# The second matrix product of a gated convolution layer, done by seven products on 2x2 blocks like the first

## The chip, the cores and the metric

The kernel runs on one core of one Trainium2 chip. The metric is the device time of one execution in microseconds, as the median of several runs. Before the change it is 1654.18 us (three runs, 1650.93 to 1654.26).

The engines are named as in the profile: PE is TensorE's matmuls and PEld its weight loads, DVE is VectorE, ACT is ScalarE, POOL is GpSimd, and SP is the engine whose queue issues nearly all DMAs here.

## The reference

One layer of a decoder trunk, batch 1, 2048 tokens, 1024 channels, all in float32:

```
shift, scale, gate = split(silu(c) @ ada_w + ada_b, 3)
h = rmsnorm(x) * (1 + scale) + shift                 # 2048 x 1024
u, gc, gb, z = split(h @ w_in, 4)                    # first product: 2048x1024 by 1024x8192
v = gc * u
y = gb * (causal_conv3(v) + conv_b) * silu(z)        # 2048 x 2048, each channel by itself
out = rmsnorm(x + gate * (y @ w_out), final_g)       # second product: 2048x2048 by 2048x1024
```

## The kernel before

Each float32 operand of a product is split into a high part in the type fp32r and a low part, what the high part leaves (`split`: ACT casts the high part, DVE subtracts). A product of two operands is three matmuls: low by high, high by high, high by low.

**First product.** It runs in two halves of the tokens (`hf` 0 and 1; 1024 tokens each). Its operands are cut into 2x2 blocks, and the four output blocks come from seven block products, not eight. The stationary side (`w`) are sums of blocks of `w_in` (`Weights`: two tiles `raw` of 512 KB for a group, the sums S1 to S4 on DVE, then seven splits). The moving side (`b`) are sums of blocks of `h`: 7 operands of 4 tiles of 512 KB, 28 tiles that stay in SBUF through a half. A group `g` (32 in a half) is seven products in the order 1, 6, 7, 5, 2, 4, 3, each of 12 matmuls of 512 columns, added up in four PSUM banks A to D: products 1 and 2 share A, 7 and 4 share D, 5 and 3 share C. `Pair.take` reads a bank when a product is done, so product 4 can't start before DVE has read D after product 7, nor product 3 before it has read C after product 5.

The moving tiles come from the pool `op`, with 33 buffers; 28 of them hold `b`. The operands of the second half are made during the first half (`make_second`, a side job of some steps, run between products) and kept in DRAM (`op_d`). They replace those of the first half during its last group, tile by tile, as each product there has used its own for the last time.

The convolution and the gating (`Mixer.finish`) write `y` to DRAM (`y_d`), channel block by channel block, with channels on partitions.

**Second product.** For each of 16 tiles of 128 tokens, `y` is loaded from `y_d` and split (`load_y`), and `mm_out` runs over 16 channel blocks, two halves of the output columns and three matmuls of 512 columns: 96 matmuls for a token tile, 1536 in all, with y as the stationary side. `w_out` is split on the way through the first two tiles and stays in SBUF. `finish` multiplies with the gate, adds x, and normalizes.

**Order.** A scheduler sets the order on each engine from dependencies, its own estimates of durations, and free buffers. `prepare(n + AHEAD)` puts the split of a stationary operand four products ahead. Engines run their instructions in order. SP's queue is in order too: a DMA that waits holds up those behind it, and each waits for the end of the one issued eight earlier (the semaphores DMAHW0 to DMAHW7).

Of the kernel before, what the change touches and what calls it, by code (L numbers as in the profile page):

```python
# [18 lines left out]
def trunk_kernel(ctx: ExitStack, tc: tile.TileContext, x, c, final_g, ada_w, ada_b,  # L19
                 w_in, conv_w, conv_b, w_out, out):  # L20

# [77 lines left out]
    op_d = dram.tile([7, KH, P, 2, CH], F32, name="op_d")  # L99
# [323 lines left out]

    ORDER = (1, 6, 7, 5, 2, 4, 3)
# [90 lines left out]
    work += [(1, g, p) for g in range(NG) for p in ORDER]  # L515
    pairs = {(0, pr.g): pr for pr in early}
# [3 lines left out]
    def load_weights(i):  # L520
        if i < 2 * NG and i not in weights:
            weights[i] = Weights(i % NG)

    def prepare(n):
        if n >= len(work):
            return
        hf, g, p = work[n]
        for d in (0, 1):
            load_weights(hf * NG + g + d)
        ready[n] = weights[hf * NG + g].operand(p)  # L530
# [98 lines left out]
    def make_second():  # L629
# [13 lines left out]
        for k in range(KH):  # L643
# [24 lines left out]
            nc.vector.tensor_sub(b12, b22, b12)
            put(7, b12)
            yield  # L670
            nc.vector.tensor_sub(b21, b21, t2)
            put(4, b21)
            yield

    wo = []

    def load_wo(j):
        r = raw()
        nc.sync.dma_start(r, w_out[j * P:(j + 1) * P, :])
        parts = [op("wo").rearrange("p h n -> p (h n)") for _ in range(2)]  # L680
        split(r, *parts, nc.vector)
        wo.append(parts)

    def begin_out():

        for j in range(2):
            load_wo(j)
            yield
# [10 lines left out]
    second = {}  # L699
    for n, (hf, g, p) in enumerate(work):  # L700
# [21 lines left out]
        if p == ORDER[-1]:  # L722
            del pairs[hf, g]
            weights.pop(hf * NG + g, None)
            if g % 2:
                jobs.insert(0, pr.mx.finish())
                del mixers[hf, g // 2]
# [9 lines left out]


    JQ = 4

    def load_y(t):

        parts = []
        for j0 in range(0, NJ, 2 * JQ):
            r = raw("yr").rearrange("p (j n) -> p j n", n=P)
            nc.sync.dma_start(r, y_d[j0:j0 + 2 * JQ, :, t * P:(t + 1) * P].rearrange("j p n -> p j n"))
            for i in range(2):
                if j0 == 0:
                    w = wp.tile([P, 2, JQ, P], F32R, name="yw", tag="w")
                    hi, lo = w[:, 0], w[:, 1]  # L750
                else:
                    hi, lo = [elp.tile([P, JQ, P], F32R, name="ye", tag="el") for _ in range(2)]
                split(r[:, i * JQ:(i + 1) * JQ], hi, lo, nc.vector)
                parts.append((hi, lo))
        return parts
# [7 lines left out]
    fg = [sp.tile([P, 512], F32, name="fg", tag="sp") for _ in range(2)]  # L763
    gate = [sp.tile([P, 512], F32, name="gate", tag="sp") for _ in range(2)]
    for h in range(2):
        nc.sync.dma_start(fg[h], final_g[h * 512:(h + 1) * 512].partition_broadcast(P))
        nc.sync.dma_start(gate[h], gate_d[h])

    def finish(t, banks):
        xa = raw("xa")  # L770
# [53 lines left out]
```

## Time and profile before

| | |
|---|---|
| median of three runs | 1654.18 us |
| the profiled execution | 1653.06 us |
| its span, first to last instruction | 1651.3 us |
| first matmul of the second product (L761) | 1290.45 us |
| last matmul starts (L761) | 1642.3 us |
| PE busy | 1622.3 us (98%) |
| DVE busy | 1036.3 us (63%) |
| ACT, POOL busy | 536.7 and 162.2 us |

A busy time of PE counts matmuls that overlap, so what a matmul costs is read as a stretch of time divided by the matmuls in it. PEclk is the share of full clock granted to TensorE (1.00 is 2.4 GHz, 0.50 is 1.2 GHz).

### The profile page before, as it was taken

What the parts mean: (1) busy time and instruction counts of PE and PEld (TensorE: products, weight loads), DVE (VectorE), ACT (ScalarE), POOL (GpSimd) and SP (SyncE); (2) the same over time, 40 slices, a digit from 0 to 9 for tenths busy, and PEclk for the clock granted to TensorE, in tenths of its full rate; (3) what the DMA queues carried; (4) which work ended last, traced back from release to release, by engine and by line L of the source; (5) the groups of instructions that cost most, each with busy time, mean ns of one, the idle gap of its engine ahead of it and who ended that gap; (6) DMA issues with size and microseconds to landing.
All of it is one profiled execution on the core that took longest, in us unless ns stands there. A gap on an engine that the chain in (4) does not pass through costs nothing.

```text
span 1651.3 us, 19240 instructions
## 1 busy us (share of the span) xinstructions
PE 1622.3 (98%) x7220; PEld 1338.0 (81%) x7220; DVE 1036.3 (63%) x1598; ACT 536.7 (33%) x893; POOL 162.2 (10%) x242
## 2 busy tenths in 40 slices
PE   9789999999999999999999999999999999999997
PEld 8577888888888888888888888888888888888886
DVE  5698776678878876676666666666666742223331
ACT  4552434344433333233333333333333520111110
POOL 2101201111111100000001001010000100000000
PEclk8999999999999999999999999999999999999999
DMA  9324324245535533932222222222223633333320
GB/s 338 97 77 128 103 90 141 90 153 170 199 93 176 199 108 94 362 88 69 65 64 64 75 79 64 71 64 70 69 84 116 222 110 102 102 102 103 102 88 27
DMA packets 213326, 190.56 MB, mean 115 GB/s; under 512 B 7651, under 2 KB 181739, under 8 KB 213234
## 3 DMA queue, kind: packets, MB, share of 16 engines
q1 hardware_dynamic: 212978, 189.31, 36.3%
q8 instruction: 56, 0.92, 0.2%
q14 instruction: 36, 0.29, 0.1%
q0 software_dynamic: 256, 0.04, 0.0%
HBM read 144.75 MB, written 44.56 MB: 115 GB/s over the span
## 4 chain that ended last, share of the span: by engine, by line
PE 76%; issue 16%; DVE 4%; DMA 1%; POOL 1%; ACT 1%; SPq 0%; POOLq 0%; DVEq 0%; ACTq 0%
PE ps L316 67%; PE ps L761 5%; PE ps L601 1%; DMA raw<-in_l_w_in_dram 1%; DVE w L164 1%; PE ps L156 1%; DVE b L164 1%; PE ps L208 0%; POOL rs L127 0%; DMA xn<-in_x_dram 0%; PE ps L104 0%; POOL t L339 0%; DVE t L338 0%; DVE s L295 0%; POOL ms L125 0%
## 5 line engine op out<-in xcount | busy, mean ns | idle before, releaser
L316 PE MATMUL ps<-b,w 128*128 128x512 f32 x5232 | 1194.2, 390 | 7.0 <-ACT hr L160 2.3
L316 PEld LDWEIGHTS ps<-b,w 128*128 128x128 f32 x5232 | 981.6, 188 | 212.8 <-ACT hr L160 3.0
L163 ACT CAST w<-raw 128x512 fp32r<-128x512 f32 x244 | 151.5, 623 | 371.4 <-PE ps L316 285.9
L163 ACT CAST w<-s 128x512 fp32r<-128x512 f32 x192 | 118.5, 619 | 204.6 <-PE ps L316 181.1
L761 PE MATMUL ps<-wo,ye 128*128 128x512 f32 x768 | 180.1, 393 | 0.0
L761 PE MATMUL ps<-wo,yw 128*128 128x512 f32 x768 | 176.9, 389 | 0.0
L164 DVE TENSOR_TENSOR w<-s,w 128x512 fp32r<-128x512 f32 x192 | 131.5, 686 | 70.8 <-ACT w L163 70.3
L164 DVE TENSOR_TENSOR w<-raw,w 128x512 fp32r<-128x512 f32 x244 | 168.2, 689 | 4.8 <-ACT w L163 4.6
L761 PEld LDWEIGHTS ps<-wo,ye 128*128 128x128 f32 x768 | 144.2, 188 | 33.3
L761 PEld LDWEIGHTS ps<-wo,yw 128*128 128x128 f32 x768 | 144.2, 188 | 30.4
L774 DVE TENSOR_TENSOR a<-ps,gate 128x512 f32<-128x512 f32 x32 | 22.0, 691 | 192.0 <-PE ps L761 191.9
L338 DVE SCALAR_TENSOR_TENSOR t<-v,cpar,t 128x512 f32<-128x512 f32 x128 | 95.8, 748 | 40.7 <-ACT t L336 39.9
L119 ACT ACTIVATE sq<-xa 128x1024 f32<-128x1024 f32 x16 | 17.0, 1060 | 274.0 <-DVE xa L775 251.5
L334 POOL COPY v<-v 128x2 f32<-128x2 f32 x32 | 21.4, 669 | 676.1 <-DVE v L386 626.2
L340 DVE TENSOR_TENSOR t<-t,gb 128x512 f32<-128x512 f32 x64 | 44.3, 692 | 56.2 <-POOL t L339 56.2
L291 DVE TENSOR_TENSOR s<-raw 128x512 f32<-128x512 f32 x64 | 44.1, 688 | 47.3 <-DMA raw<-in_l_w_in_dram 47.3
L415 DVE TENSOR_TENSOR u<-ps,u 128x512 f32<-128x512 f32 x58 | 40.0, 690 | 40.2 <-PE ps L316 40.2
L375 ACT COPY u<-ps 128x512 f32<-128x512 f32 x58 | 34.0, 586 | 94.6 <-PE ps L316 94.6
L336 ACT ACTIVATE t<-v,cpar 128x512 f32<-128x512 f32 x64 | 52.1, 815 | 5.2 <-DVE v L421 3.6
L601 PE MATMUL ps<-b,we 128*128 128x512 f32 x144 | 48.5, 468 | 5.2 <-DVE keep L375 5.2
L339 POOL TENSOR_TENSOR t<-t,sz 128x512 f32<-128x512 f32 x29 | 40.2, 1388 | 122.1 <-DVE t L338 98.0
L339 POOL TENSOR_TENSOR t<-t,u 128x512 f32<-128x512 f32 x29 | 39.4, 1358 | 118.4 <-issue 71.0
(99 smaller groups left out, 964.1 us busy)
## 6 DMA issues: line engine op xcount, KB each, us to landing
raw<-in_l_w_in_dram SPq DMA_DIRECT2D x128, 512.0 KB, 4.1
y_d<-t SPq DMA_DIRECT2D x64, 256.0 KB, 2.4
yr<-y_d SPq DMA_DIRECT2D x32, 512.0 KB, 4.9
op_d<-b SPq DMA_DIRECT2D x28, 512.0 KB, 3.3
b<-op_d SPq DMA_DIRECT2D x28, 512.0 KB, 9.1
xn<-in_x_dram SPq DMA_DIRECT2D x16, 512.0 KB, 5.3
ada<-in_l_ada_w_dram SPq DMA_DIRECT2D x32, 256.0 KB, 6.0
raw<-in_l_w_out_dram SPq DMA_DIRECT2D x16, 512.0 KB, 4.3
```

Of the source, the lines that this page charges most:

```text
L163: nc.scalar.copy(hi, src)
L164: eng.tensor_sub(lo, src, hi.bitcast(F32))
L291: nc.vector.tensor_add(d, a21, a22)
L316: nc.tensor.matmul(ps, lhsT=w[:, i, k * P:(k + 1) * P], rhs=b[k][:, m], start=first and k == 0 and n == 0, stop=k == KH - 1 and n == 2, sk ...
L336: nc.scalar.activation(t, v[:, 2:], AF.Identity, bias=cpar[:, j, 3:4], scale=cpar[:, j, 2:3])
L338: nc.vector.scalar_tensor_tensor(t, v[:, w:CH + w], cpar[:, j, w:w + 1], t, ALU.mult, ALU.add)
L339: nc.gpsimd.tensor_mul(t, t, self.sz[ci])
L340: nc.vector.tensor_mul(t, t, self.gb[ci])
L375: (eng or nc.scalar.copy)(a, self.ps["A"])
L415: nc.vector.tensor_add(self.u, ps, self.u)
L601: nc.tensor.matmul(pr.ps["A"], lhsT=wk[k][i][:, e * P:(e + 1) * P], rhs=b[:, m], start=k == 0 and n == 0, stop=k % KH == KH - 1 and n == 2 ...
L761: nc.tensor.matmul(ps, lhsT=a, rhs=b, start=j == 0 and n == 0, stop=j == NJ - 1 and n == 2)
```

## The change

The second product gets the same seven products. Rows of blocks are pairs of token tiles (8 pairs, `OutPair`), columns of blocks the halves of the 1024 output channels. The 2048 channels summed over are taken in two passes, named `hf` 2 and 3, of 1024 channels each. The stationary side are sums of blocks of `y`, loaded from `y_d` by `Weights`. The moving side are sums of blocks of `w_out`, already multiplied with the gate: `make_wo`, a side job during `hf` 1, makes 28 tiles for each pass and keeps them in DRAM (`op_d2`, `op_d3` in the rows below). A pass has 8 x 7 x 12 = 672 matmuls of 512 columns.

`OutPair.take` adds the banks into two tiles `xa` of 128 x 1024, which begin as x (pass 2) or as the sum so far (pass 3). Pass 2 stores them to `acc_d`; pass 3 loads them from there, normalizes and stores the output. The tiles `xa` and `fg` come from the pool `op`. The moving tiles are now replaced three times instead of once: in the last group of `hf` 0, of `hf` 1 and of pass 2.

The core of the diff:

```diff
-    op_d = dram.tile([7, KH, P, 2, CH], F32, name="op_d")
+    op_d = [None] + [dram.tile([7, KH, P, 2, CH], F32, name=f"op_d{i}") for i in range(1, 4)]
+    acc_d = dram.tile([S // P, P, D], F32, name="acc_d")
...
-        def __init__(self, g, n=2):
+        def __init__(self, hf, g):
             self.a = []
-            for q, j in rows(g)[:n]:
+            for i in range(2):
                 r = raw()
-                nc.sync.dma_start(r.rearrange("p (k n) -> p k n", k=KD), w_view[:, :, q, j, :])
+                if hf < NH:
+                    q, j = rows(g)[i]
+                    src = w_view[:, :, q, j, :]
+                else:
+                    src = y_d[(hf - NH) * KD:(hf - NH + 1) * KD, :, (2 * g + i) * P:(2 * g + i + 1) * P]
+                    src = src.rearrange("j p n -> p j n")
+                nc.sync.dma_start(r.rearrange("p (k n) -> p k n", k=KD), src)
...
+    class OutPair(Pair):
+        def __init__(self, hf, g):
+            self.ps = {}
+            self.ts = (2 * g, 2 * g + 1)
+            self.last = hf == NH + 1
+            self.xa = []
+            for t in self.ts:
+                a = op("xa", F32)
+                src = acc_d[t] if self.last else x[t * P:(t + 1) * P, :]
+                nc.sync.dma_start(a.rearrange("p h n -> p (h n)"), src)
+                self.xa.append(a)
+        def add(self, i, h, b):
+            a = self.xa[i][:, h]
+            nc.vector.tensor_add(a, b, a)
+        def take(self, p, ps):
+            if p == 1:
+                self.u = el("u")[:, :CH]
+                nc.scalar.copy(self.u, ps)
+            elif p == 6:
+                nc.vector.tensor_add(self.u, ps, self.u)
+            elif p == 7:
+                self.add(1, 1, ps)
+                self.add(1, 1, self.u)
+            elif p == 5:
+                self.add(1, 1, ps)
+            elif p == 2:
+                self.add(0, 0, ps)
+            elif p == 4:
+                self.add(1, 0, ps)
+                self.add(1, 0, self.u)
+                self.finish(1)
+            else:
+                self.add(0, 1, self.u)
+                self.add(0, 1, ps)
+                self.finish(0)
+        def finish(self, i):
+            a, t = self.xa[i], self.ts[i]
+            if not self.last:
+                nc.sync.dma_start(acc_d[t], a.rearrange("p h n -> p (h n)"))
+                return
+            parts = []
+            for h in range(2):
+                ss = small.tile([P, 1], F32, name="ss", tag="ss")
+                nc.scalar.activation(el("sq")[:, :CH], a[:, h], AF.Square, scale=float(D) ** -0.5, accum_out=ss)
+                parts.append(ss)
+            nc.gpsimd.tensor_add(parts[0], parts[0], parts[1])
+            rs = rstd(parts[0])
+            for h in range(2):
+                nc.vector.scalar_tensor_tensor(a[:, h], a[:, h], rs, fg[0][:, h], ALU.mult, ALU.mult)
+                nc.sync.dma_start(out[t * P:(t + 1) * P, h * CH:(h + 1) * CH], a[:, h])
...
+    work += [(hf, g, p) for hf in (2, 3) for g in range(S // P // 2) for p in ORDER]
+    sequence = list(dict.fromkeys((hf, g) for hf, g, _ in sorted(work, key=lambda w: w[:2])))
...
+    def put_operands(hf, k, b11, b21, b12, b22):
+        def put(p, src):
+            t = split_op(src)
+            nc.sync.dma_start(op_d[hf][p - 1, k], t.bitcast(F32))
+
...
+    def make_wo():
+        gate = op("gate", F32)
+        nc.sync.dma_start(gate, gate_d.rearrange("h p n -> p h n"))
+        for hf in (2, 3):
+            for k in range(KH):
+                ab = [op("wr", F32) for _ in range(2)]
+                for i, a in enumerate(ab):
+                    j = (hf - NH) * KD + i * KH + k
+                    nc.sync.dma_start(a.rearrange("p h n -> p (h n)"), w_out[j * P:(j + 1) * P, :])
+                yield
+                yield
+                for a in ab:
+                    nc.vector.tensor_mul(a, a, gate)
+                    yield
+                (b11, b12), (b21, b22) = [(a[:, 0], a[:, 1]) for a in ab]
+                yield from put_operands(hf, k, b11, b21, b12, b22)
...
-    second = {}
+    ops = [bops, {}, {}, {}]
+    last = {hf: g for hf, g in sequence}
...
+        if (hf, g, p) == (3, 0, 1):
+            fg.append(op("fg", F32))
+            nc.sync.dma_start(fg[0].rearrange("p h n -> p (h n)"), final_g.partition_broadcast(P))
+        pr.run(p, ready.pop(n), ops[hf])
         if (hf, g, p) == (0, 2 * EU, 1):
             jobs.append(side())
-        if (hf, g, p) == (1, NG - 3, 1):
-            jobs.append(begin_out())
-        if hf == 0 and g == NG - 1:
-            i = ORDER.index(p)
-            for q in ORDER[i:i + 1]:
-                second[q] = []
-                for k in range(KH):
-                    t = op("b")
-                    nc.sync.dma_start(t.bitcast(F32), op_d[q - 1, k])
-                    second[q].append(t)
+        elif (hf, g, p) == (1, 0, 1):
+            jobs.append(make_wo())
+        if hf < 3 and g == last[hf]:
+            ops[hf + 1][p] = []
+            for k in range(KH):
+                t = op("b")
+                nc.sync.dma_start(t.bitcast(F32), op_d[hf + 1][p - 1, k])
+                ops[hf + 1][p].append(t)
...
-    def mm_out(ps, parts, j, h):
-        hi, lo = [a[:, j % JQ, :] for a in parts[j // JQ]]
-        wh, wl = [a[:, h * 512:(h + 1) * 512] for a in wo[j]]
-        for n, (a, b) in enumerate(((lo, wh), (hi, wh), (hi, wl))):
-            nc.tensor.matmul(ps, lhsT=a, rhs=b, start=j == 0 and n == 0, stop=j == NJ - 1 and n == 2)
...
```

What the change moves, at the opening of a round of operands. First SP's queue as the operands of the second half of tokens are reloaded, before the change: the tiles b of the last two products (L720; the last six of 28), the stores of y, and the next stationary tiles raw. The names behind "waits" are semaphores: an engine's, or DMAHW0 to DMAHW7 for the DMA issued eight earlier or for the one that fills a tile.

```order
L720 DMA b_5522<-op_d_104 128x1024 [waits DMAHW0_49,PE_49]
L720 DMA b_5524<-op_d_104 128x1024 [waits DMAHW1_49,PE_49]
L720 DMA b_5543<-op_d_104 128x1024 [waits DMAHW2_49,PE_49]
L720 DMA b_5545<-op_d_104 128x1024 [waits DMAHW3_49,PE_49]
L720 DMA b_5547<-op_d_104 128x1024 [waits DMAHW4_49,PE_49]
L720 DMA b_5549<-op_d_104 128x1024 [waits DMAHW5_49,PE_49]
L342 DMA y_d_101<-t_5570 128x512 [waits DMAHW6_49,DVE_49]
L342 DMA y_d_101<-t_5614 128x512 [waits DMAHW7_49,DVE_49]
L278 DMA raw_5621<-in_l0_w_in_dram 128x8x128 [waits DMAHW0_49,Activation_49]
L278 DMA raw_5623<-in_l0_w_in_dram 128x8x128 [waits DMAHW1_49,Activation_49]
```

Nothing that VectorE needs for the new group's PSUM banks stands behind the tiles b here. Now SP's queue as those of pass 3 are reloaded, with the change (L799; the last eight of 28). L478 stores the last sums of pass 2, L445 loads the sums xa for the first pair of pass 3, L789 the scale of the final norm.

```order
L799 DMA b_11499<-op_d3_106 128x1024 [waits DMAHW0_49,PE_49]
L799 DMA b_11501<-op_d3_106 128x1024 [waits DMAHW1_49,PE_49]
L799 DMA b_11503<-op_d3_106 128x1024 [waits DMAHW2_49,PE_49]
L799 DMA b_11505<-op_d3_106 128x1024 [waits DMAHW3_49,PE_49]
L478 DMA acc_d_107<-xa_11344 128x1024 [waits DMAHW4_49,DVE_49]
L799 DMA b_11525<-op_d3_106 128x1024 [waits DMAHW5_49,PE_49]
L799 DMA b_11527<-op_d3_106 128x1024 [waits DMAHW6_49,PE_49]
L799 DMA b_11529<-op_d3_106 128x1024 [waits DMAHW7_49,PE_49]
L799 DMA b_11531<-op_d3_106 128x1024 [waits DMAHW0_49,PE_49]
L445 DMA xa_11536<-acc_d_107 128x1024 [waits DMAHW1_49,PE_49]
L445 DMA xa_11538<-acc_d_107 128x1024 [waits DMAHW2_49,PE_49]
L789 DMA fg_11540<-in_final_g_dram 128x1024 [waits DMAHW3_49,PE_49]
```

The loads of xa, which VectorE must have before it can read PSUM in the new pass, stand behind all 28 tiles b, and two stores of 512 KB stand between these.

VectorE as the second half of tokens opens, before: its reads of D (ps_5598, L401) and C (ps_5628, L403) in the first group; v and t are tiles in SBUF that it writes.

```order
L401 TENSOR_TENSOR v_5611<-ps_5598,u_5567 128x512 [waits DMAHW0_49,DVE_49,PE_49]
L164 TENSOR_TENSOR w_5642<-s2_5645,w_5642 128x512 [waits Activation_49]
L338 SCALAR_TENSOR_TENSOR t_5614<-v_5274,cpar_100,t_5614 128x512 [waits DMAHW2_49,DMAHW1_49,Activation_49]
L301 TENSOR_TENSOR s2_5645<-raw_5443,s2_5645 128x512 [waits DVE_49]
L338 SCALAR_TENSOR_TENSOR t_5614<-v_5274,cpar_100,t_5614 128x512 [waits DVE_49]
L403 TENSOR_TENSOR v_5611<-ps_5628,v_5611 128x512 [waits PE_49]
L340 TENSOR_TENSOR t_5614<-t_5614,gb_5433 128x512 [waits Pool_49]
```

Both reads wait for PE, and write tiles that no DMA fills. VectorE as pass 3 opens, with the change: splits (L167), then the first reads of A, D and C of the first pair (ps_11542, ps_11578, ps_11600; L450).

```order
L167 TENSOR_TENSOR w_11721<-raw_11425,w_11721 128x512 [waits Activation_49]
L167 TENSOR_TENSOR w_11738<-s2_11617,w_11738 128x512 [waits Activation_49]
L450 TENSOR_TENSOR xa_11536<-ps_11542,xa_11536 128x512 [waits DMAHW1_49]
L450 TENSOR_TENSOR xa_11536<-u_11555,xa_11536 128x512
L450 TENSOR_TENSOR xa_11538<-ps_11578,xa_11538 128x512 [waits DMAHW2_49]
L450 TENSOR_TENSOR xa_11538<-u_11555,xa_11538 128x512 [waits DVE_49]
L450 TENSOR_TENSOR xa_11538<-ps_11600,xa_11538 128x512 [waits DVE_49]
```

The first additions now wait for the DMAs of xa (DMAHW1, DMAHW2), and the reads of D and C stand behind them.

PE as the second half opens, before: product 2 of the first group ends (ps_5554), then product 4 into D (ps_5598).

```order
L316 MATMUL ps_5554<-b_5496,w_5551 128x512 [waits DMAHW4_49]
L316 MATMUL ps_5554<-b_5496,w_5551 128x512 x2
L316 MATMUL ps_5554<-b_5498,w_5551 128x512 [waits DMAHW5_49]
L316 MATMUL ps_5554<-b_5498,w_5551 128x512 x2
L316 MATMUL ps_5598<-b_5518,w_5577 128x512 [waits DMAHW6_49,DVE_49]
L316 MATMUL ps_5598<-b_5518,w_5577 128x512 x2
```

Product 4 follows product 2 of the same group. PE as pass 3 opens, with the change: product 5 of the second pair (ps_11764), then product 4 of the first pair into D (ps_11578).

```order
L325 MATMUL ps_11764<-b_11446,w_11667 128x512 x3
L325 MATMUL ps_11764<-b_11448,w_11667 128x512 x3
L325 MATMUL ps_11764<-b_11450,w_11667 128x512 x3
L325 MATMUL ps_11578<-b_11499,w_11557 128x512 [waits DMAHW0_49,DVE_49]
L325 MATMUL ps_11578<-b_11499,w_11557 128x512 x2
L325 MATMUL ps_11578<-b_11501,w_11557 128x512 [waits DMAHW1_49]
```

The scheduler has put products of the second pair ahead of products 4 and 3 of the first. Counted from the first matmul of the pass, product 4 of the first pair begins with matmul 108; in program order it would be 60.

## Rows read from the trace of the kernel before

**Rows 1.** The page: busy time and share of each engine.

```profile
PE 1622.3 (98%) x7220; PEld 1338.0 (81%) x7220; DVE 1036.3 (63%) x1598; ACT 536.7 (33%) x893; POOL 162.2 (10%) x242
```

**Rows 2.** Five stretches (us): busy us and count of each engine, clock, DMA share, GB/s.

```profile
core 0: us, PE busy (x) PEld busy (x) DVE busy (x) ACT busy (x) POOL busy (x), PEclk, DMA share, GB/s
400.00:560.00 160.00, 160.00 (x707) 132.53 (x707) 129.79 (x205) 61.61 (x104) 16.98 (x20) 1.00 0.52 175
700.00:1270.00 570.00, 570.00 (x2516) 472.01 (x2515) 385.40 (x602) 185.28 (x302) 53.62 (x75) 1.00 0.25 74
1300.00:1640.00 340.00, 340.00 (x1485) 278.46 (x1484) 107.90 (x159) 56.79 (x96) 11.84 (x30) 1.00 0.35 105
663.00:672.00 9.00, 9.00 (x41) 7.44 (x41) 4.21 (x8) 2.98 (x5) 0.00 (x0) 1.00 0.97 331
672.00:696.00 24.00, 24.00 (x108) 19.87 (x107) 17.26 (x27) 7.91 (x13) 3.58 (x5) 1.00 1.03 402
```

**Rows 3.** PE in order of time, at 1290 us: start, length, instruction, count.

```profile
1288.64 1.98 PE L316 MATMUL ps<-b,w 128*128 128x512 f32 x8
1290.45 4.92 PE L761 MATMUL ps<-wo,yw 128*128 128x512 f32 x21
```

**Rows 4.** All engines after the last matmuls: start, length, instruction, [idle before it].

```profile
1641.58 1.09 PE L761 MATMUL ps<-wo,ye 128*128 128x512 f32 x4
...
1642.01 1.39 DVE L774 TENSOR_TENSOR a<-ps,gate 128x512 f32<-128x512 f32 x2 [15.64 <-PE ps L761]
1643.31 1.28 DVE L775 TENSOR_TENSOR xa<-xa,a 128x512 f32<-128x512 f32 x2
1644.77 1.06 ACT L119 ACTIVATE sq<-xa 128x1024 f32<-128x1024 f32 x1 [20.81 <-DVE xa L775]
...
1646.31 0.57 POOL L127 TENSOR_TENSOR rs<-ms,nhalf 128x1 f32<-128x1 f32 x1
1646.91 1.41 DVE L779 SCALAR_TENSOR_TENSOR xa<-xa,rs,fg 128x512 f32<-128x512 f32 x2 [2.31 <-POOL rs L127]
```

**Rows 5.** The page: costly groups: busy us, mean ns | idle before, releaser.

```profile
L164 DVE TENSOR_TENSOR w<-s,w 128x512 fp32r<-128x512 f32 x192 | 131.5, 686 | 70.8 <-ACT w L163 70.3
...
L338 DVE SCALAR_TENSOR_TENSOR t<-v,cpar,t 128x512 f32<-128x512 f32 x128 | 95.8, 748 | 40.7 <-ACT t L336 39.9
...
L415 DVE TENSOR_TENSOR u<-ps,u 128x512 f32<-128x512 f32 x58 | 40.0, 690 | 40.2 <-PE ps L316 40.2
```

**Rows 6.** SP issues, 663 to 697 us: start, length of the row, DMA, count.

```profile
663.01 4.52 SPq L720 DMA_DIRECT2D b<-op_d  x7
667.62 0.49 SPq L278 DMA_DIRECT2D raw<-in_l_w_in_dram  x1
668.21 20.55 SPq L720 DMA_DIRECT2D b<-op_d  x16
```

**Rows 7.** PE over the same stretch.

```profile
656.66 48.71 PE L316 MATMUL ps<-b,w 128*128 128x512 f32 x214
```

**Rows 8.** Loads b issued at 663 us: issue to landing.

```profile
DMA to landing us min/median/max: 4.8/5.1/5.4
```

**Rows 9.** Loads b issued at 687 and 688 us: issue to landing.

```profile
DMA to landing us min/median/max: 10.1/10.1/10.1
```

**Rows 10.** Who PE waited for: us in total, times, longest.

```profile
PE ps L601 <- DVE keep L375: 5.2, 1, 5.2
```

**Rows 11.** PE around that wait: us, busy (count), granted clock, DMA share, GB/s.

```profile
48.00:50.00 2.00, 0.92 (x5) 1.00 0.03 13
...
52.00:54.00 2.00, 0.00 (x0) 0.53 0.77 223
...
56.00:58.00 2.00, 2.00 (x9) 0.50 0.00 0
58.00:60.00 2.00, 2.00 (x10) 0.77 0.00 0
```

More of the change, by code (lines that the diff above doesn't have):

```diff
@@ L520, in load_weights @@
     def load_weights(i):
-        if i < 2 * NG and i not in weights:
-            weights[i] = Weights(i % NG)
+        if i < len(sequence) and sequence[i] not in weights:
+            weights[sequence[i]] = Weights(*sequence[i])
     def prepare(n):
@@ L527, in prepare @@
         hf, g, p = work[n]
+        i = sequence.index((hf, g))
         for d in (0, 1):
-            load_weights(hf * NG + g + d)
-        ready[n] = weights[hf * NG + g].operand(p)
+            load_weights(i + d)
+        ready[n] = weights[hf, g].operand(p)
     def now(f, *args):
@@ L668, in make_second @@
[L668 to L688, printed above, removed]
+            yield from put_operands(1, k, b11, b21, b12, b22)
@@ new lines, in put_operands @@
+    def put_operands(hf, k, b11, b21, b12, b22):
+        def put(p, src):
+            t = split_op(src)
+            nc.sync.dma_start(op_d[hf][p - 1, k], t.bitcast(F32))
+        put(1, b11)
+        yield
+        put(2, b21)
+        yield
+        put(3, b22)
+        yield
+        t2 = el("t2")[:, :CH]
+        nc.vector.tensor_sub(b11, b12, b11)
+        put(5, b11)
+        yield
+        nc.vector.tensor_sub(t2, b22, b11)
+        put(6, t2)
+        yield
+        nc.vector.tensor_sub(b12, b22, b12)
+        put(7, b12)
+        yield
+        nc.vector.tensor_sub(b21, b21, t2)
+        put(4, b21)
+        yield
@@ L706, in trunk_kernel @@
         if (hf, g) not in pairs:
-            pairs[hf, g] = Pair(hf, g)
+            pairs[hf, g] = Pair(hf, g) if hf < NH else OutPair(hf, g)
         pr = pairs[hf, g]
-        pr.run(p, ready.pop(n), second if hf else bops)
+        if (hf, g, p) == (3, 0, 1):
+            fg.append(op("fg", F32))
+            nc.sync.dma_start(fg[0].rearrange("p h n -> p (h n)"), final_g.partition_broadcast(P))
+        pr.run(p, ready.pop(n), ops[hf])
         if (hf, g, p) == (0, 2 * EU, 1):
             jobs.append(side())
-        if (hf, g, p) == (1, NG - 3, 1):
-            jobs.append(begin_out())
-        if hf == 0 and g == NG - 1:
-            i = ORDER.index(p)
-            for q in ORDER[i:i + 1]:
-                second[q] = []
-                for k in range(KH):
-                    t = op("b")
-                    nc.sync.dma_start(t.bitcast(F32), op_d[q - 1, k])
-                    second[q].append(t)
+        elif (hf, g, p) == (1, 0, 1):
[6 more added lines that the diff above has]
+                ops[hf + 1][p].append(t)
         if p == ORDER[-1]:
             del pairs[hf, g]
-            weights.pop(hf * NG + g, None)
-            if g % 2:
+            weights.pop((hf, g), None)
+            if hf < NH and g % 2:
                 jobs.insert(0, pr.mx.finish())
@@ L736, in trunk_kernel @@
             pass
[L739 to L755, printed above, removed]
@@ L769, in finish @@
-    def finish(t, banks):
-        xa = raw("xa")
-        nc.sync.dma_start(xa, x[t * P:(t + 1) * P, :])
-        for h in range(2):
-            a = el("a")[:, :512]
-            nc.vector.tensor_mul(a, banks[h], gate[h])
-            nc.vector.tensor_add(xa[:, h * 512:(h + 1) * 512], xa[:, h * 512:(h + 1) * 512], a)
-        rs = rstd(square_sum(xa, raw("sq")))
-        for h in range(2):
-            a = xa[:, h * 512:(h + 1) * 512]
-            nc.vector.scalar_tensor_tensor(a, a, rs, fg[h], ALU.mult, ALU.mult)
-            nc.sync.dma_start(out[t * P:(t + 1) * P, h * 512:(h + 1) * 512], a)
@@ L782, in trunk_kernel @@
-    NT = S // P
-    blocks = [[0, 1]] + [[t] for t in range(2, NT)]
-    ys = {t: load_y(t) for t in blocks[0]}
-    for b, ts in enumerate(blocks):
-        banks = {t: [bank() for _ in range(2)] for t in ts}
-        for j in range(NJ):
-            if j >= len(wo):
-                load_wo(j)
-            for t in ts:
-                for h in range(2):
-                    mm_out(banks[t][h], ys[t], j, h)
-            if j == NJ // 2 and b + 1 < len(blocks):
-                for t in blocks[b + 1]:
-                    ys[t] = load_y(t)
-        for t in ts:
-            finish(t, banks[t])
```

25 lines of the change are left out of this document (4 added, 21 removed).

## The prediction

> **What bounds the kernel now.** I read the page's busy times first: PE 98% of the span, DVE 63% [rows 1]. Shares are averages, so next the stretches: from 700 to 1270 us, the second half of the first product, PE is never idle and 2516 matmuls take 570 us, 0.2266 us each; from 1300 to 1640 us, the second product, 1485 take 340 us, 0.2290 each, PE never idle either [rows 2]. So in both stages the end is set by the number of matmuls. Then PE in order of time, for where the second product begins (1290.45 us) [rows 3] and where it ends (1641.58 + 1.09 = 1642.67) [rows 4]: 352.2 us for 1536 matmuls. From there to the end of the span are 1651.30 - 1642.67 = 8.6 us of adding, normalizing and storing. The other views serve the two places where the change can lose: the reload of moving tiles [rows 6 to 9], and what a stall of PE costs in clock [rows 10, 11].
>
> **What the change removes: matmuls.** 2 passes of 672 are 1344 for 1536. They have the form of the first product's (same `product`, same tiles w and b), so I price them by its row: 1344 x 0.2266 = 304.5 us, for 352.2: 47.7 us less. By the second product's own row they would be 1344 x 0.2290 = 307.8. I take the first, since the code is the same, and keep 3.3 us as a bound.
>
> **The tail.** Before: two multiplications and two additions on VectorE, one square sum of 1024, two steps on POOL, two scalings [rows 4]. After the last product one addition is left (0.7), a square sum of one half (0.6 for 1.06), the accumulator and three POOL steps (some 1.6 together); from the first scaling to the end of the span the same 1651.30 - 1646.91 = 4.4. Sum 7.3 us, 1.3 less.
>
> **What it adds during the second half of the first product.** `make_wo` puts 8 x (2 multiplications + 4 sums + 7 splits) = 104 instructions on VectorE, and about as many casts as splits on ACT. This lies beside matmuls if VectorE keeps pace. The row of 400 to 560 us is the measure: there another side job makes operands in just these steps, VectorE runs 205 instructions in 160 us, 24.4 in the 19.04 us of a group (84 matmuls), and PE does 707 matmuls, 0.2263 us each: nothing lost [rows 2]. From 700 to 1270 us it runs 602 in 570, 20.1 a group; 104 more, the wide ones counted twice, over some 27 groups make it 24.5. The same density, so I take 0.5 us; bounds 0 and 4.
>
> **What it adds in the passes.** A pair needs 7 splits, 4 sums and 9 additions on VectorE: 20 instructions in pass 2, and 4 scalings more in pass 3: 24, still under the 24.4 that hid. So in the middle of a pass the price is nothing, and the cover is the four products of lead that `prepare` gives. Gone is the splitting of `w_out` and y.
>
> **What it adds where operands change.** This is the one wait that I expect to see. Before, the reload happens once, around 681 us (662.1 below, and a group more). The last group of the first half begins 24 matmuls after 656.66 us, at 656.66 + 24 x 48.71 / 214 = T = 662.1 [rows 7]; its first tile is free 3 matmuls later, and the first load goes out at 663.0 [rows 6]. It lands 4.8 us later at 667.8 [rows 8]. The 24th (7 + 1 raw + 16) goes out at 688.4 and lands 10.1 us later at 698.5 [rows 6, 9]. So load k lands at T + 5.7 + 1.335 x (k - 1). That the row of PE has 214 matmuls in 48.71 us with no break shows that this was just in time [rows 7].
>
> Opening of pass 2: five tiles are loaded ahead as before, so the two xa are loads 25 and 26, the last at T + 39.1. VectorE needs them for three additions, 2 us, before product 4 of the first pair, which the order places 113 matmuls into the pass: T + (84 + 113) x 0.2266 = T + 44.6. Room of 3.5 us; 0.5 us for small waits.
>
> Opening of pass 3: the tiles xa hold the spare buffers, so one tile goes ahead, not five, and two stores of sums stand between the loads. The xa are loads 31 and 32. Two stores of the pair before also stand ahead of the first load: 2 x 1.3 us, most of it behind T; I add 2. Load 32 lands at T + 5.7 + 41.4 + 2 = T + 49.1, its addition from D ends 0.8 later, at T + 49.9. Product 4 waits for it, and the order has it 108 matmuls into the pass: T + (84 + 108) x 0.2266 = T + 43.5. **PE stalls 6.4 us.** Queued on VectorE behind the waiting addition are the splits of the third pair, which PE needs two products later; they come in time. Bounds: 0 (the stores land before T and a few loads are quicker), and 14 at 1.58 us a load, the 331 GB/s of 663 to 672 us in place of the 402 of 672 to 696 [rows 2].
>
> The Trainium skill's page "DMA: Bandwidth & Descriptors", section "Where 436 GB/s comes from", says that between HBM and SBUF the HBM side binds, at about 358 GB/s; the trace differs, with 402 GB/s over 24 us [rows 2], and the measurement decides. By the page a load would take 1.46 us, the stall would be 10.4, and the time 1619, an estimate from it.
>
> A stall costs clock too. PE waited 5.2 us once [rows 10]; the granted clock was 0.53 from 52 to 54 us, 0.50 to 58 and 0.77 from 58 to 60 (1.2 GHz until about 58.9), while PE was at work again from 54.1 [rows 10, 11]: 4.8 us at half speed, 2.4 lost. I add these 2.4. The page "TensorE: Matmul & The Clock Gate", section "Why this matters for your kernels", has the same rule, that a gap between bursts of matmuls sets the clock back to half, and the trace agrees; without it the sum would be 1612.6.
>
> **The sum.** 1290.45 + 0.5 + 0.5 + 304.5 + 6.4 + 2.4 + 7.3 = 1612.1 us of span, 1651.3 before. The profiled execution took 1653.06, 1.8 more than its span: 1613.9. The median of the runs, 1654.18, is 1.1 above it: **1615 us**, 39 us or 2.4% less.
>
> **Rivals.**
> *No stall at pass 3* (the loads come in time): 1615 - 8.8 = 1606. For it: at the reload before, nothing was lost [rows 7]. Against: xa stands eight loads further back in the queue than the last tile did.
> *The reload is dearer.* At 1.58 us a load, xa in pass 2 lands at T + 45.2, 2.5 us too late, and in pass 3 the stall is 14.1: 1615 + 2.5 + 7.7 = 1625. For it: 331 GB/s in the first 9 us. Against: that stretch was filling up.
> *The matmuls keep the rate of the old second product*: 1615 + 3.3 = 1618.
> *Slower: VectorE sets the pace of the passes.* It runs in order, and its waits would stand in a row: in pass 3 for a pair 20 x 0.69 + 4 x 0.75 = 16.8 us busy, 7 x 0.37 = 2.6 for ACT's casts (70.8 / 192), 7 x 0.69 = 4.8 for products (40.2 / 58) [rows 5], and 2 x 2.3 for the square sums and POOL [rows 4]: 28.8 us, 9.8 over PE's 19.0, 78 us in 8 pairs; in pass 2 21.2, 17 us in all. That would be 1615 + 95 = 1710. It decides from 39 / 16 = 2.4 us more than PE's time for a mean pair. For it: one more wait for POOL a token tile. Against: back to back these start 0.60 apart (205 in 160 us with splits and waits among them, and PE lost nothing [rows 2]), and the splits are four products ahead.
>
> **How the numbers follow.** 1615 with 1609 to 1621 around it: 0.60. No stall: 0.15. Dearer reload: 0.10. The old rate: 0.08. VectorE: 0.07, of which about 0.02 ends under the time before. The range must take in no stall without small losses (1604) and the dear reload with 4 us more in the first product (1629): **1603 to 1630**, with some 0.12 outside, mostly above. About 0.2% is what a measurement of this kernel can tell from no change, so faster 0.93, same 0.02, slower 0.05.
>
> **What would show it.** PE: 1344 matmuls at 0.2266 us in the new stage, and one break of some 6 us about 24 us into pass 3 that ends on VectorE's xa, followed by clock 0.50 for some 5 us; none over 1 us at pass 2; 84 matmuls in 19 us elsewhere; the new stage begins within 1 us of 1290. VectorE: some 80% busy in pass 3. Wrong if PE waits for w or for PSUM reads in the middle of pass 3 (VectorE too slow), if the first product ends later than 1294, or if the break at pass 3 lies elsewhere, or is absent.

## The result, and the profile after

The changed kernel takes **1613.5 us** (median of 4 runs, 1613.19 to 1614.43) beside 1653.35 us (4 runs) for the kernel before on the same chip: ratio 0.9762, 95% interval 0.9745 to 0.9779, so 39.9 us or 2.4% less. The prediction said 1615 us, 1603 to 1630. The profiled execution has a span of 1612.6 us in 1614.43.

Busy time and share of each engine after, beside [rows 1]:

```profile
PE 1578.2 (98%) x7028; PEld 1301.9 (81%) x7028; DVE 1208.4 (75%) x1878; ACT 593.6 (37%) x1029; POOL 175.8 (11%) x258
```

192 matmuls fewer (7220 to 7028), 280 VectorE instructions more, and PE as full as before. The stretches that answer to [rows 2] (us; busy us and count of PE, PEld, DVE, ACT, POOL; granted clock, DMA share, GB/s): the second half of the first product with `make_wo` beside it, most of pass 2, the middle of pass 3.

```profile
700.00:1270.00 570.00, 569.14 (x2511) 470.95 (x2510) 452.19 (x704) 211.99 (x355) 60.62 (x75) 1.00 0.43 142
1300.00:1440.00 140.00, 140.00 (x619) 115.91 (x618) 97.75 (x154) 35.73 (x59) 1.62 (x1) 1.00 0.65 228
1500.00:1600.00 100.00, 100.00 (x442) 82.66 (x441) 78.69 (x126) 35.24 (x79) 13.38 (x30) 1.00 0.42 143
```

In both passes PE is never idle and a matmul takes 140 / 619 = 0.2262 and 100 / 442 = 0.2262 us by these counts; start to start over each whole stretch of the trace it is 0.2267. VectorE runs 126 instructions in 100 us of pass 3, 24.0 in 19.04 us. Waits of PE from 1290 us to the end (us in total, times, longest): there is one.

```profile
PE ps L325 <- DVE xa L450: 5.7, 1, 5.7
```

Where it lies, on PE, then VectorE, then SP, in order of time (start, length, instruction, count, [idle before it, and what ended it]):

```profile
1462.70 5.83 PE L325 MATMUL ps<-b,w 128*128 128x512 f32 x25
1474.19 6.13 PE L325 MATMUL ps<-b,w 128*128 128x512 f32 x18 [5.66 <-DVE xa L450]
```

```profile
1472.15 0.69 DVE L450 TENSOR_TENSOR xa<-ps,xa 128x512 f32<-128x512 f32 x1 [4.96 <-DMA xa<-acc_d]
...
1473.44 0.69 DVE L450 TENSOR_TENSOR xa<-ps,xa 128x512 f32<-128x512 f32 x1
```

```profile
1456.29 4.06 SPq L799 DMA_DIRECT2D b<-op_d  x4
1461.31 1.58 SPq L445 DMA_DIRECT2D xa<-acc_d  x2
1464.56 0.33 SPq L789 DMA_DIRECT2D fg<-in_final_g_dram  x1
```

Pass 3 begins at 1443.88 us. PE stops after matmul 108 of it, before product 4 of the first pair, which needs bank D; VectorE reads D at 1473.44, behind the addition that waits for the first tile `xa`; both `xa` were asked for after all 28 tiles `b`. Counted from T, the first matmul of the last group of pass 2 (1424.84), PE goes on at T + 49.35.

What the stall costs in clock (us, PE busy (count), and so on; granted clock in the third column from the right):

```profile
1470.00:1472.00 2.00, 0.00 (x0) 0.00 (x0) 0.00 (x0) 0.00 (x0) 0.00 (x0) 0.77 1.01 401
...
1474.00:1476.00 2.00, 1.81 (x4) 1.50 (x5) 1.52 (x3) 0.00 (x0) 0.00 (x0) 0.50 1.22 301
1476.00:1478.00 2.00, 2.00 (x6) 1.57 (x5) 0.69 (x1) 0.62 (x1) 0.00 (x0) 0.52 1.04 364
1478.00:1480.00 2.00, 2.00 (x10) 1.60 (x10) 1.72 (x3) 0.00 (x0) 0.00 (x0) 1.00 1.08 356
```

The granted clock falls while PE stands still (0.77 from 1470 to 1472) and is 0.50 (1.2 GHz) until about 1478. Nine matmuls start from 1474.19 to 1478, 0.43 us apart, where 17 would have fit. Against a spacing of 0.2267 us the break loses 5.8 us and the slow matmuls behind it 1.9, 7.7 together; small delays later in the pass add 0.4, 8.1 in all.

The end, beside [rows 4]:

```profile
1603.70 0.84 PE L325 MATMUL ps<-b,w 128*128 128x512 f32 x3
...
1604.58 0.69 DVE L450 TENSOR_TENSOR xa<-ps,xa 128x512 f32<-128x512 f32 x1 [1.30 <-PE ps L325]
...
1606.16 0.60 POOL L485 TENSOR_TENSOR ss<-ss 128x1 f32<-128x1 f32 x1 [0.23 <-ACT sq L483]
1606.74 3.18 SPq L489 DMA_DIRECT2D out_dram<-xa  x4
1606.85 0.61 POOL L128 TENSOR_SCALAR ms<-ss 128x1 f32<-128x1 f32 x1
1607.54 0.57 POOL L130 TENSOR_TENSOR rs<-ms,nhalf 128x1 f32<-128x1 f32 x1
1608.14 1.42 DVE L488 SCALAR_TENSOR_TENSOR xa<-xa,rs,fg 128x512 f32<-128x512 f32 x2 [0.77 <-POOL rs L130]
```

1612.65 - 1604.54 = 8.1 us lie behind the last matmul.

### The profile page after: what moved, and what is told of

Read it like the earlier page. It is cut to its first block, busy times and chain, and to the rows that moved or that the text cites. A ratio compares the mean times of both kernels' runs of the same rounds, so it can differ in the third digit from the quotient of the medians.

```text
span 1612.6 us, 19711 instructions
## 1 busy us (share of the span) xinstructions
PE 1578.2 (98%) x7028; PEld 1301.9 (81%) x7028; DVE 1208.4 (75%) x1878; ACT 593.6 (37%) x1029; POOL 175.8 (11%) x258
## 3 DMA queue, kind: packets, MB, share of 16 engines
q1 hardware_dynamic: 233554, 264.81, 48.6%
## 4 chain that ended last, share of the span: by engine, by line
PE 82%; DVE 8%; DMA 4%; issue 3%; ACT 1%; POOL 1%; SPq 0%; POOLq 0%; DVEq 0%; ACTq 0%
PE ps L325 79%; DMA raw<-in_l_w_in_dram 2%; DVE w L167 2%; PE ps L673 2%; DMA b<-op_d 1%; DVE b L167 1%; PE ps L159 1%; POOL t L348 1%; DMA xa<-acc_d 1%; DVE t L347 1%; DVE s L300 1%; DVE s L304 0%; DVE raw L307 0%; DVE gate_m L232 0%; DMA xn<-in_x_dram 0%
## 5 line engine op out<-in xcount | busy, mean ns | idle before, releaser
L325 PE MATMUL ps<-b,w 128*128 128x512 f32 x6576 | 1503.4, 390 | 15.1 <-DVE xa L450 5.7
L325 PEld LDWEIGHTS ps<-b,w 128*128 128x128 f32 x6576 | 1235.9, 188 | 275.9 <-DVE xa L450 6.6
L166 ACT CAST w<-raw 128x512 fp32r<-128x512 f32 x308 | 191.1, 622 | 433.1 <-PE ps L325 349.0
L167 DVE TENSOR_TENSOR w<-s,w 128x512 fp32r<-128x512 f32 x240 | 164.1, 685 | 81.7 <-ACT w L166 81.2
L167 DVE TENSOR_TENSOR w<-raw,w 128x512 fp32r<-128x512 f32 x308 | 213.6, 694 | 15.3 <-ACT w L166 15.0
L347 DVE SCALAR_TENSOR_TENSOR t<-v,cpar,t 128x512 f32<-128x512 f32 x128 | 95.5, 747 | 21.9 <-ACT t L345 20.5
L450 DVE TENSOR_TENSOR xa<-ps,xa 128x512 f32<-128x512 f32 x80 | 54.7, 686 | 33.9 <-PE ps L325 28.7
L310 DVE TENSOR_TENSOR s<-raw,s 128x512 f32<-128x512 f32 x80 | 55.9, 699 | 0.7
L304 DVE TENSOR_TENSOR s<-s,raw 128x512 f32<-128x512 f32 x80 | 54.9, 686 | 0.9
L307 DVE TENSOR_TENSOR raw<-raw 128x512 f32<-128x512 f32 x80 | 54.6, 682 | 0.0
L424 DVE TENSOR_TENSOR u<-ps,u 128x512 f32<-128x512 f32 x58 | 39.8, 686 | 19.1 <-PE ps L325 19.1
L402 DVE TENSOR_TENSOR u<-ps,u 128x512 f32<-128x512 f32 x58 | 39.6, 683 | 4.5 <-PE ps L325 4.5
```

Of the source, the lines that this page charges most:

```text
L166: nc.scalar.copy(hi, src)
L167: eng.tensor_sub(lo, src, hi.bitcast(F32))
L304: nc.vector.tensor_sub(d, s1, a11)
L307: nc.vector.tensor_sub(d, a11, a21)
L310: nc.vector.tensor_sub(d, a12, d)
L325: nc.tensor.matmul(ps, lhsT=w[:, i, k * P:(k + 1) * P], rhs=b[k][:, m], start=first and k == 0 and n == 0, stop=k == KH - 1 and n == 2, sk ...
```

## The experiments

Times are compared by their ratio to the kernel before, which ran beside each of them (1651.8 to 1652.4 us); the changed kernel ran a second time too. From the first matmul of pass 2 to the last of pass 3 (called the passes below) the trace gives a second measure: 312.6 us in the changed kernel, 304.5 with no break (1343 x 0.2267).

### The changed kernel again

> The changed kernel as it is, beside the others of this call on one chip: 1612 to 1615 us, ratio 0.976 to the kernel before.

1613.09 us, ratio 0.9761 (0.9744 to 0.9777); passes 312.4 us, break 5.22 us. But pass 2 begins at 1288.47 us here and at 1291.54 in the first profile, with the same kernel. Two stretches at the start, first profile and then this one, show where:

```profile
0.00:160.00 160.00, 142.83 (x684) 116.27 (x685) 121.68 (x187) 75.88 (x135) 22.23 (x44) 0.94 0.51 163
```

```profile
0.00:160.00 160.00, 144.38 (x696) 116.95 (x696) 123.04 (x191) 76.59 (x136) 24.29 (x45) 0.95 0.52 163
```

12 matmuls more in the first 160 us, 2.7 us, at a granted clock of 0.95 for 0.94. From 160 to 1280 us the two have 4952 and 4951 matmuls. It need not be the chip: four of the kernels below, run together on one chip with the first product written the same, begin pass 2 at 1288.6, 1288.8, 1291.2 and 1291.7 us, with a granted clock of 0.96, 0.96, 0.93 and 0.94 in the first 160 us. So the start of the kernel scatters by some 3 us, along with the clock granted there, and small effects are better read from the passes.

### Does the number of matmuls set the time?

```diff
     class OutPair(Pair):
+        def run(self, p, w, bops):
+            ps, first = self.target(p)
+            if p == 1:
+                product(ps, w, bops[p], True, True)
+            product(ps, w, bops[p], first, True)
+            self.take(p, ps)
```

> Product 1 of each of the 16 pairs of the second product is computed twice into the same bank (the first sum is overwritten): 16 x 12 = 192 more matmuls, 1536 as in the kernel before, with nothing else added. Theory (the number of matmuls times 0.2266 us is what sets the time): +192 x 0.2266 = +43.5 us, less up to 2.7 us of the break in pass 3, in which the repeated product gives the residual loads more time: 1654 to 1657 us, no faster than the kernel before. Rival (the changed second product is held by VectorE, at 24 instructions in a pair, or by DMA): the repeat lies in their shadow, below +20 us, under 1635 us.

1650.53 us, ratio 0.9987 (0.9976 to 0.9998): with 1536 matmuls again, nearly all of the gain is gone. That is 37 us more than the changed kernel, below the 41 to 43.5 expected, because nearly all of the break in pass 3 goes. All that PE still waits for from 1290 us on:

```profile
PE ps L325 <- DVE xa L457: 0.5, 1, 0.5
```

43.5 - 8.1 + 1.4, what the two kernels' passes lose beside their matmuls, is 36.8. Three repeated products lie between T and product 4 of the first pair (one in the last group, two in the first two pairs), 8.2 us, while the second `xa` lands only 1.1 us later (T + 49.7 for T + 48.6): 7.1 us more cover, where I had counted 2.7. Both `xa` are now in before PE gets to product 4 (T + 51.7). The wait that is left is another one: VectorE's additions stand behind a split that waits for ScalarE's cast.

```profile
1493.99 0.69 DVE L167 TENSOR_TENSOR w<-s,w 128x512 fp32r<-128x512 f32 x1 [2.03 <-ACT w L166]
1494.60 0.68 DVE L457 TENSOR_TENSOR xa<-ps,xa 128x512 f32<-128x512 f32 x1
```

Nothing hides the repeat, so outside the opening of pass 3 neither VectorE nor DMA sets the pace.

### How much room VectorE has

```diff
+            if p in (6, 5, 2):          # second kernel: (1, 6, 7, 5, 2, 4)
+                nc.vector.tensor_add(el("ex")[:, :CH], self.xa[0][:, 0], self.xa[0][:, 1])
```

> Three more VectorE additions of a 128x512 tile in each of the 16 pairs, after products 6, 5 and 2, into a scratch tile that nobody reads: 27 instead of 24 VectorE instructions in a pair of pass 3. At the 0.60 us from start to start at which such instructions follow each other, 27 x 0.60 = 16.2 us of the 19.04 us that 84 matmuls take. Theory (VectorE still lies beside TensorE with room): 0 to +1.5 us. Rival (VectorE is already near its bound, by durations 24 x 0.69 = 16.6 us and with its waits no room): 16 x 3 x 0.3 to 0.6 = +14 to +29 us.

> Six more VectorE additions in each pair, one after each product but the last: 30 in a pair of pass 3, 18.0 us at 0.60 us each, of 19.04 us. Theory: the cover is nearly used up; 0 to +10 us, the loss in pass 3 alone, as short waits PE <- DVE at the openings of pairs, while pass 2 with 16 + 6 = 22 loses nothing. Rival (VectorE near its bound): +29 us or more, in both passes.

1618.1 us (ratio 0.9793, 0.9774 to 0.9812) and 1636.68 us (0.9898, 0.9879 to 0.9918), or +0.3% and +1.4% on the changed kernel: about 5 and 22 us (the passes take 318.7 and 333.7 us, 6 and 21 more). Both are over my ranges, and under the rival's. The middle of pass 3, with three and then with six more:

```profile
1500.00:1600.00 100.00, 99.69 (x438) 81.49 (x437) 87.30 (x142) 39.00 (x91) 15.73 (x36) 1.00 0.45 150
```

```profile
1500.00:1600.00 100.00, 92.38 (x396) 73.51 (x395) 90.06 (x147) 32.33 (x76) 12.31 (x30) 1.00 0.47 154
```

With 27 a pair PE does 438 matmuls in 100 us there for 442, 0.9 us lost; with 30 it does 396, 10.4 us lost, and VectorE, 90% busy, gets no more than 147 done. So the edge in the middle of a pass lies between. I had put it higher: an instruction takes 100 / 147 = 0.68 us there, its waits included, for the 0.60 I had counted, and 30 of them need 20.4 us of the 19.04. And I missed the openings. With three more, pass 2 takes 154.8 us for 152.3, and the loss is two breaks at matmuls 108 and 120, products 4 and 3 of the first pair; with six more it takes 159.8, all lost by matmul 145. There the reads of banks come behind the extra additions and behind gating steps left from the first product (L347), and PE, which runs two pairs at once, waits for them. VectorE with three more, before the break that ends at 1319.27 us:

```profile
1316.66 1.29 DVE L474 TENSOR_TENSOR ex<-xa 128x512 f32<-128x512 f32 x2
1317.87 0.75 DVE L347 SCALAR_TENSOR_TENSOR t<-v,cpar,t 128x512 f32<-128x512 f32 x1
1318.53 0.68 DVE L450 TENSOR_TENSOR xa<-ps,xa 128x512 f32<-128x512 f32 x1
```

But the additions moved the scheduler's order too. In pass 2 of both of these kernels product 4 begins with matmul 108; in the changed kernel PE's wait for VectorE stands at matmul 113, as the prediction had it. So the loss in pass 2 is that of the additions and of an order 5 matmuls (1.1 us) tighter, and their shares aren't told apart. VectorE has some room between openings and little in them.

### The break in pass 3: the place of `xa` in SP's queue

```diff
+        if (hf, g, p) == (2, last[2], 7):
+            pairs[3, 0] = OutPair(3, 0)
+        if (hf, g, p) == (3, 0, 1):            # second kernel only
+            pairs[3, 1] = OutPair(3, 1)
         if hf < 3 and g == last[hf]:
             ops[hf + 1][p] = []
```

> The two residual tiles of pair (3,0) are asked for some 5 us earlier, ahead of the last four reloads of moving tiles instead of among them; nothing is left out. Theory (the 5.7 us break in pass 3 is the place of the residual loads in SP's queue): the break at matmul 108 of the pass goes. The residual tiles of pair (3,1), which stand in the same queue behind pair (3,0)'s stores, are then the next late thing, one pair on, so that of the 5.7 us only 0 to 2 come back: 1611.5 to 1613.5 us. Rival (the opening is short of bandwidth as a whole): a break of about 5 us stays before matmul 108, now ended by a reloaded moving tile, PE <- DMA b, at product 7, 5 or 2 of pair (3,0), and the time stays at 1613.5.

> As the run before, and the residual tiles of pair (3,1) too are asked for one pair early, at the second group of pass 3. Theory (place in the queue): no break before matmul 108; VectorE's own order (scalings of pair (3,0), which wait for POOL, ahead of its reads of a finished bank of pair (3,1)) leaves a break of about 3 us near matmul 144 of the pass; time 1609 to 1611 us, ratio to the changed kernel about 0.998. Rival (bandwidth of the whole opening): the break of 5 to 6 us before matmul 108 stays, PE <- DMA b, 1613 us or more.

1608.6 us (ratio 0.9733, 0.9718 to 0.9748) and **1607.61 us** (0.9730, 0.9713 to 0.9747); passes 308.9 and 308.25 us. The break at matmul 108 is gone in both, though the same bytes are moved, so the rival, bandwidth of the whole opening, falls. SP's queue of the first of them shows the move:

```profile
1425.02 2.84 SPq L801 DMA_DIRECT2D b<-op_d  x5
1428.12 1.48 SPq L445 DMA_DIRECT2D xa<-acc_d  x2
1430.61 4.87 SPq L801 DMA_DIRECT2D b<-op_d  x4
```

The expectation had misjudged how far they move: not 5 us, but to the head of the reload, some 30 us earlier. It was wrong too on what comes back (3.7 us of the passes for 0 to 2) and on what is late next. Not the `xa` of the second pair stop PE, but the engines' order. PE, ScalarE and VectorE of the second kernel, at matmuls 132 and 144 of the pass:

```profile
1473.13 3.02 PE L325 MATMUL ps<-b,w 128*128 128x512 f32 x12 [2.01 <-ACT u L455]
1477.24 5.06 PE L325 MATMUL ps<-b,w 128*128 128x512 f32 x21 [1.09 <-DVE xa L450]
```

```profile
1469.79 0.63 ACT L483 ACTIVATE sq<-xa 128x512 f32<-128x512 f32 x1 [6.27 <-DVE xa L450]
...
1471.89 0.63 ACT L483 ACTIVATE sq<-xa 128x512 f32<-128x512 f32 x1
...
1472.52 0.57 ACT L455 COPY u<-ps 128x512 f32<-128x512 f32 x1
```

```profile
1472.39 1.41 DVE L488 SCALAR_TENSOR_TENSOR xa<-xa,rs,fg 128x512 f32<-128x512 f32 x2 [0.54 <-POOL rs L130]
1474.58 1.41 DVE L488 SCALAR_TENSOR_TENSOR xa<-xa,rs,fg 128x512 f32<-128x512 f32 x2 [0.77 <-POOL rs L130]
...
1476.51 0.68 DVE L450 TENSOR_TENSOR xa<-ps,xa 128x512 f32<-128x512 f32 x1
```

ScalarE's copy of the second pair's bank A stands behind four squares of the first pair, though it has sat idle 6.27 us before them; VectorE's reads stand behind scalings that wait for POOL. Of the 8.1 us, 4.4 come back and 3.8 are lost at these two waits.

The first of the two kernels has the same wait of 2.0 us for ScalarE at matmul 132 and none at 144, but 1.7 us of low clock follow it, and in the second kernel none. The same stretch in the first and then in the second (granted clock third from the right):

```profile
1474.00:1476.00 2.00, 2.00 (x6) 1.52 (x6) 1.25 (x2) 0.00 (x0) 0.64 (x2) 0.50 0.71 264
```

```profile
1474.00:1476.00 2.00, 2.00 (x10) 1.44 (x8) 1.43 (x3) 0.13 (x1) 0.54 (x1) 1.00 1.17 317
```

So the length of a break alone doesn't tell whether the clock falls; what decides it isn't shown.

### Taking those two orders away

First the scalings of a pair put off until the next pair's product 5 is taken; then the squares put off too, until its product 1 is copied.

```diff
             rs = rstd(parts[0])
-            for h in range(2):
-                nc.vector.scalar_tensor_tensor(a[:, h], a[:, h], rs, fg[0][:, h], ALU.mult, ALU.mult)
-                nc.sync.dma_start(out[t * P:(t + 1) * P, h * CH:(h + 1) * CH], a[:, h])
+            def scale():
+                ...
+            if t < 14:
+                late.append(scale)      # called in take: p == 5 of the next pair
+            else:
+                scale()
```

> As the run before, and the two scalings and stores of each token tile of the last pass wait until the following pair's product 5 has been taken (the last pair's are not put off). Theory: the break that VectorE's order leaves in the second pair goes too; with 5.7 us of idle time and about 2 us of the lower granted clock gone, and 0 to 1 us new at the reloads, 1605.5 to 1607.5 us. Rival (VectorE's order plays no part, the opening is short of bandwidth): as the run before, 1609 us or more.

> As the run with the residual tiles of pairs (3,0) and (3,1) asked for early, which kept two breaks of 2.4 and 1.5 us from start to start (ScalarE's copy of a product-1 bank behind four squares of the pair before; VectorE's reads behind scalings that wait for POOL). Now the squares and POOL's steps of a pair are put behind the next pair's copy of its product 1, and the scalings behind its product 5; the last pair's are not put off. Theory (these two orders are all that is left): both breaks go, 3.2 us less from the first matmul of pass 2 to the last, 305 us there, and 1604 to 1606 us. Rival (the buffers that the put-off tiles hold make the residual tiles of pair (3,2) late): a new break of 2 us or more in the third pair, 1607 us or more.

Neither did what I expected: 1608.37 us (ratio 0.9734, 0.9715 to 0.9753) and 1612.12 us (0.9756, 0.9740 to 0.9772). In the first the passes take 307.6 us: the copy behind the squares still costs 2.4 us, the scalings 0.8 for 1.4. In the second the copy is early and its break gone, but a longer one stands at matmul 144:

```profile
1478.73 3.78 PE L325 MATMUL ps<-b,w 128*128 128x512 f32 x8 [5.76 <-DVE xa L450]
```

```profile
1473.61 1.41 DVE L495 SCALAR_TENSOR_TENSOR xa<-xa,rs,fg 128x512 f32<-128x512 f32 x2
1476.06 1.41 DVE L495 SCALAR_TENSOR_TENSOR xa<-xa,rs,fg 128x512 f32<-128x512 f32 x2 [1.04 <-POOL rs L130]
1477.39 1.28 DVE L450 TENSOR_TENSOR xa<-ps,xa 128x512 f32<-128x512 f32 x2
```

The scheduler, which orders by its own estimates, has still put the scalings ahead of the second pair's reads, and PE waits for the second of the two additions behind them. PE came 2.4 us earlier to a wait that ended 2.3 us later in the pass than before: the first pair's last product now ends with matmul 143 of the pass, not 131, so VectorE's last addition for that pair starts at 1473.00, 32.9 us into the pass for 30.2, and the squares, POOL's steps and the scalings follow it. The break, now longer, brought the low clock back: 8.1 us lost. The rival's cause, late `xa` of the third pair, isn't seen either.

The kernel with the two early loads alone has the lowest median, and its interval just meets that of the changed kernel (0.9730 for 0.9762), while its passes are 4.1 to 4.4 us shorter in the trace. By the times it can't be told from the kernel with the scalings put off, whose passes are 0.6 us shorter still and which began pass 2 at 1291.2 us in its trace, not 1288.6. So the first step did a part of what I expected, the second undid it. The passes could still give 3 to 4 us, and which order of the engines gives it stays open.

### Why the old second product was slower per matmul

The prediction priced the new matmuls at 0.2266 us and kept the old 0.2290 as a bound. In the kernel before, the 48 matmuls of a token tile whose stationary tile lies in the weight pool (`yw`) start 0.2271 us apart, the 48 from the element pool (`ye`) 0.2313. The last token tile, with no load beside it, has the difference too (0.2268 and 0.2304). Three kernels, all made from the one before:

```diff
-        return elp.tile([P, CH + CW - 1], F32, name=name, tag="el")
+        return elp.tile([P, 528], F32, name=name, tag="el")[:, :CH + CW - 1]
```

> The kernel before, with one size changed: the slots of the element pool are 528 floats (2112 bytes) wide instead of 514 (2056 bytes); the same instructions on the same shapes. In the kernel before the 768 matmuls of the second product whose stationary tile lies in that pool (ye) follow each other at 0.2313 us and the 768 others (yw) at 0.2271. Theory (the slot's address is what costs the 0.004 us): ye falls to 0.227, 768 x 0.0042 = 3.2 us less than the kernel before, about 1650 us. Rival (something else that goes with the second half of each tile's products): no change.

```diff
-                if j0 == 0:
+                if j0 != 0:                 # third kernel: if j0 == 0 or t > 1:
                     w = wp.tile([P, 2, JQ, P], F32R, name="yw", tag="w")
```

> The kernel before, with the two kinds of stationary tile of the second product swapped: the first 8 of the 16 channel tiles of each token tile now lie in the element pool (ye), the last 8 in the weight pool (yw). Theory (slot): the 0.231 us goes with ye, now in the first half of each token tile's matmuls, and the time stays within 0.2%. Rival (the place in time, beside the loads and splits of the next token tile): the second half, now yw, is the slower one.

> The kernel before, with the stationary tiles of the second product from the third token tile on all in the weight pool (yw); the first two token tiles keep both kinds. Theory (what costs 0.004 us is that the tile lies in the element pool): 14 x 48 = 672 matmuls go from 0.2312 to 0.2271 us, 2.8 us less, ratio 0.9983 to the kernel before. Rival (it is the pairing of two halves of a token tile, or the length of its run): no change within 0.5 us.

The wider slot did not help: ratio 0.9991 (0.9982 to 1.0001), `ye` at 0.2305 us. With the halves swapped the slow spacing went with `ye` (0.2311 for 0.2270; the one run's 1661.8 us holds a new wait of 5.8 us in the first tiles, `PE <- DVE ye`, so its time says nothing of this). With all in the weight pool the ratio is 0.9978 (0.9968 to 0.9988), 3.6 us less where 2.8 were expected. PE by form from 1340 to 1630 us (busy us, mean ns of one), in the kernel before and in this one:

```profile
L761 PE MATMUL ps<-wo,yw 128*128 128x512 f32 x643 | 148.3, 389 | 0.0
L761 PE MATMUL ps<-wo,ye 128*128 128x512 f32 x624 | 146.4, 393 | 0.0
```

```profile
L761 PE MATMUL ps<-wo,yw 128*128 128x512 f32 x1281 | 290.5, 389 | 0.0
```

So the pool in which the stationary tile lies is shown as the cause; the pitch of its slots alone moves little (0.2305 for 0.2313). In the element pool the high and the low part are two tiles, in the weight pool the halves of one, and which of the pools' differences counts wasn't tried. Some 3 to 4 of the change's 40 us are therefore a matter of where stationary tiles lie, and not of the seven products.

## Why the prediction was right

- **What bounds it** held: matmuls, one behind the other, in both passes. Repeating product 1 lost 37 of the 40 us again.
- **Matmuls**: 304.5 us predicted at 0.2266; the trace has 1343 x 0.2267 = 304.5 and the breaks. The choice of the first product's row over the second's was right, but its reason, "the code is the same", was not the cause. The tiles' pool was.
- **Second half of the first product**: 0.5 us predicted. One break, `PE <- DVE v L410`, of 0.86 us, and 2511 matmuls for 2516 in 570 us: 1.1 us. VectorE runs 704 instructions there, 23.5 a group; 24.5 were forecast.
- **Opening of pass 2**: 0.5 us predicted, none found. The second `xa` landed at T + 39.4, 39.1 predicted, but the room was some 0.5 us and not 3.5: VectorE's additions stand behind a split that waits for ScalarE's cast, so its read of D ends at 1316.6 us, and matmul 113 starts at 1317.2. The working had counted the loads and left out VectorE's order.
- **Opening of pass 3**: break of 6.4 us before product 4, ending on `xa` at T + 49.9; measured 5.7 us, same place, same releaser, T + 49.35. The second `xa` landed at T + 48.6 (issued 1462.58, 10.8 us), predicted T + 49.1. The clock's part was 1.9 us, predicted 2.4.
- **Tail**: 7.3 us predicted, 8.1 measured. The term that was too small is the accumulator and the three POOL steps: 2.2 us, 2.0 of them from 1606.16 to the scaling, where 1.6 were counted.
- **Start**: pass 2 was put at 1291.0 us; the two profiles have 1291.5 and 1288.5, both outside the "within 1 us of 1290" given as a sign. So a good part of how closely 1612.1 us of span met 1612.6 is luck: the start alone scatters by 3 us.
- **Rivals**: no stall is refuted by the trace, the dearer reload too (the second `xa` landed 0.5 us before the forecast, not 7.7 after it), and the old rate by 0.2267. VectorE as the pace is refuted for this kernel, but its distance was overrated: six additions more in each pair cost 22 us.

## What to carry to other kernels

Count the instructions of the engine that bounds a stage, and price them by the row of a stage with the same operands in the same pools. At an opening, write down the queue of the DMA engine and the order of VectorE and ScalarE; two loads that stood behind a reload of 28 tiles stopped PE for 5.7 us here, and asked for ahead of it they made PE wait for no other load. Then expect the next order to show: of 8.1 us, 4.4 came back, and taking away one of the two waits behind it made the other one longer. An edit that adds or moves instructions can also move the scheduler's order on PE, so read that order again before a loss is put down to the edit alone.

## What the hardware showed that I had not expected

The same matmul with 512 columns, with nothing idle before it, starts 0.2313 us after the one before where its stationary tile lies in the element pool's slots, and 0.2271 (0.2267 in a long run) where it lies in the weight pool's 4096-byte slots. It differs from slot to slot, and token tiles repeat in a cycle of six (0.2321, 0.2304, 0.2320, 0.2295, 0.2319, 0.2312, and again from 0.2321). A pitch of 2112 bytes for 2056 left it at 0.2305. What about the slots does it stays open.
